# A list scheduler for the w_in stage: other durations, merges of both directions together, and another order of the last gMLP blocks

## The chip, the cores and the metric

The kernel runs on one NeuronCore of a Trainium2 chip, as one program. The metric is the device time of one execution in microseconds (us), here the median of three runs. Everything is computed in fp32; large products are made of three products of split operands (type fp32r, high and low part), small ones are plain fp32.

## The reference, cut to what matters

The reference is one layer of a backbone for 640 tokens (512 latent, 128 context) with a width of 2048. The change lies in the part that makes `p = h @ w_in` and turns its columns into the inputs of a later scan and into the gated spatial unit.

```python
h = _rmsnorm(x, lp['norm1_g']) * (1.0 + sc1) + sh1
p = h @ lp['w_in']
o_a, s_fin = _rwkv7_bidir(shift_fn(p[..., :C_SHIFT], lp['mu_shift']), s0, lp)
o_b = _chunk_gmlp(jax.nn.gelu(p[..., C_SHIFT:]), lp)
x = x + g1 * (jnp.concatenate([o_a, o_b], axis=-1) @ lp['w_out'])
...
def _chunk_gmlp(p, lp):
    u, v = jnp.split(p, 2, axis=-1)
    v = v.astype(F32).reshape(B, T // CHUNK, CHUNK, N_GROUPS_B, HEAD_B)
    mean = jnp.mean(v, axis=-1, keepdims=True)
    vc = v - mean
    v = vc * lax.rsqrt(jnp.mean(vc * vc, axis=-1, keepdims=True) + LN_EPS) * lp['gmlp_ln_g'] + lp['gmlp_ln_b']
    s = jnp.einsum('gij,bnjgd->bnigd', lp['w_spatial'], v) + lp['b_spatial'].T[:, :, None]
    return (u * s.reshape(B, T, D_B)).astype(dtype)
```

`_rwkv7_bidir` is a delta-rule scan over the tokens, forward and backward, for 16 heads of 64. The kernel does it in chunks of 64 tokens: within a chunk it needs the inverse of a triangular 64x64 matrix for each head, direction and chunk. `_chunk_gmlp` has 8 groups of 128 columns for the value `v` and 8 for the gate `u`.

## The kernel before, in words

The program has four stages: the first modulation and norm with the first three column blocks of w_in (up to some 150 us); the rest of w_in with everything that hangs on its columns (the stage of this change); the scan over chunks together with the product with w_out; and the feed-forward part.

**The w_in stage.** The columns of w_in come in blocks of 128. Three are done earlier; 40 remain: for each of 8 pairs of heads the blocks r, v and k, and for each of 8 gMLP groups a value block (`take_gv`) and a gate block (`take_gu`). A block is 96 "wide" products of 128x128 by 320 columns (`wides`, from line 1180): 16 parts of the contraction, two halves of the tokens, three products each (high by high, high by low, low by high). `fetch` loads raw weights on SP, three buffers ahead; `parted` splits them into `hi` on ACT and `lo` on DVE. A finished block is copied to an SBUF buffer `praw` (a ring of four) and given to the queue of its kind.

**What hangs on a block.** `take_r`, `take_v`, `take_k` shift the tokens and build the decays, `R` and `X`; `take_v` also writes the turned values through a tile `vt` to DRAM. `tail` makes the chunk products (`pG`, 64x64 tiles), `turned_x` and `first_z` (`pXT`, `pW`) write more of the scan's records `d_S`. `solve` inverts 16x16 triangles on DVE; `merge` (line 1030) puts them together to 32x32 and then to 64x64 in five steps for each direction: three `pblk` products, `pM` and `pT`, each a group of 20 or 40 products of 32x32 tiles on PE, followed by copies on ACT or additions on DVE. There are 8 merges, so 80 such steps. The result `TF` is stored by a DMA on the POOL queue. `take_gv` does the gelu, turns the value block and `w_spatial`, normalises over 128 columns (mean, variance, root, gain and bias) into `vt`; `take_gu` does the gelu of the gate block, multiplies `vt` by the turned `w_spatial` (`psp`), adds the bias, multiplies and stores `d_o`. `mod_all` makes the remaining modulation vectors in 64 groups of four products (`pm`, 128x32 tiles), paced by the count of wides.

**Who sets the order.** `Lister` (from line 231) writes the order of every engine's instructions at build time. Each queue is a task that yields operations; an `Op` has a cost in microseconds (from line 89). `Lister` keeps a clock for every engine, works out when a task's next operation would be ready, and emits the one that could start first. On PE (`pick`) the wides are the filling. A small product of the full 128x128 shape is taken as soon as it has been ready for SLACK; one of another tile shape interrupts the wides if two small ones are ready for SLACK, or if one has waited for PATIENCE (2 us). Off the full shape, others that are ready for SLACK go along. A change of shape costs 0.195 us on the list's clock. Priorities: r, v, k, tails 2, merges 3, solve 4, gMLP (`qB`, one queue, one block after another) and `mod_all` 5. The list fixes only the order; on the chip each instruction waits for its inputs.

**At the end of the stage.** The main list ends with the last wide. What is left in the queues is emitted by `plan.run(last=True)` outside the hand-made order, where the framework orders it among the first instructions of the next stage. That stage starts with transposes of x (`pxT`), the first scan steps (`swap`, `w_ps`, `u_ps`, `s_ps`, `y_ps`) and products with w_out. PSUM has four slots for small products in this stage (`slots`); `slots.pair` waits for two.

Of the kernel before, what the change touches and what calls it, by code (L numbers as in the profile page):

```python
# [19 lines left out]
P = 128  # L20
# [5 lines left out]
CH = 64  # L26
# [26 lines left out]
SLACK = 1.0  # L53
# [35 lines left out]
class Op:  # L89
# [14 lines left out]
    def __init__(self, eng, name, fn, args, kw):  # L104
# [126 lines left out]
class Lister:  # L231
# [10 lines left out]
    def add(self, gen, prio):  # L242
        self.tasks.append(Task(gen, prio))
# [39 lines left out]
    def pick(self, eng, tasks):  # L283
        now = self.clock[eng]
        c = [(self.ready(t.item), t.rank(), i, t) for i, t in enumerate(tasks)]
        if eng == "PE":
# [8 lines left out]
            if small and (not wide or len(small) >= TOGETHER or now - min(small)[0] >= PATIENCE):  # L295
# [23 lines left out]
def flow_step(ctx: ExitStack, tc, x_prompt, x_sample, state_rwkv, c, c_ctx, w_mod, b_mod,  # L319
# [420 lines left out]
    pairs = [Pair() for _ in range(NPAIR)]  # L740

# [6 lines left out]
    def take_v(pr, p, read):  # L748
# [198 lines left out]
    def take_gv(vv, g, read):  # L947
        lng, lnb, wsp = (gs.tile([P, P], F32, tag=n, name=n) for n in ("lng", "lnb", "wsp"))
        yield oQ.dma_start(lng, gmlp_ln_g[0, g].partition_broadcast(P))
        yield oQ.dma_start(lnb, gmlp_ln_b[0, g].partition_broadcast(P))  # L950
# [17 lines left out]
        va = gs.tile([P, NT], F32, name="gva")  # L968
# [61 lines left out]
    def merge(p, d2):  # L1030
# [6 lines left out]
        for h in range(2):  # L1037
            base = 64 * (1 - h)
            for d in range(2):
                yield oS.copy(A1_[base:base + 16, d, :, 16:32], GB[d][base:base + 16, :, 16:32])  # L1040
                yield oS.copy(A1_[base + 32:base + 48, d, :, 16:32], GB[d][base + 32:base + 48, :, 48:64])
        for d in range(2):
            GBd = GB[d]
            TF = bp.tile([P, NCH, CH], F32, tag="TF", name="TF")
            for h in range(2):
                yield oG.memset(TF[hi32(h), :, 0:32], 0.0)
            Tn, TT, A1 = TB[:, d, :, 0, :], TB[:, d, :, 1, :], A1_[:, d]

            def blk(lhs, rhs, rows=range(4)):
                ps = slots.tile([P, NCH, 32], F32, "pblk")  # L1050
                four = []
                for cc in range(NCH):
                    for a_ in rows:
                        s = slice(32 * a_, 32 * a_ + 32)
                        four.append(oT.matmul(ps[s, cc, :], lhs[s, cc, :], rhs[s, cc, :], start=True, stop=True,
                                             tile_position=(32 * a_, 32 * a_)))
                return ps, four

            M1 = bp.tile([P, NCH, 32], F32, tag="M1", name="M1")
            yield slots.free  # L1060
            ps, four = blk(A1, Tn)
            yield four
            yield oS.copy(M1, ps)
            slots.done(ps)

            yield slots.free
            ps, four = blk(TT, M1, (0, 2))
            yield four
            for h in range(2):
                yield oV.tensor_add(Tn[lo32(h)], ps[lo32(h)], Tn[lo32(h)])  # L1070
            slots.done(ps)
            yield slots.free
            ps, four = blk(M1, TT)
            yield four
            for h in range(2):
                yield oV.tensor_add(TF[lo32(h), :, 0:32], ps[lo32(h)], TT[lo32(h)])
                yield oV.tensor_add(TF[hi32(h), :, 32:64], ps[hi32(h)], TT[hi32(h)])
            slots.done(ps)
            M2 = bp.tile([P, NCH, 32], F32, tag="M1", name="M2")
            yield slots.free  # L1080
            ps = slots.tile([P, NCH, 32], F32, "pM2")
            yield [oT.matmul(ps[hi32(h), cc, :], GBd[lo32(h), cc, 32:64], Tn[lo32(h), cc, :],
                            start=True, stop=True, tile_position=(64 * (1 - h), 64 * (1 - h) + 32))
                   for cc in range(NCH) for h in range(2)]
            for h in range(2):
                yield oS.copy(M2[hi32(h), :, :], ps[hi32(h), :, :])
            slots.done(ps)
            yield slots.free
            ps = slots.tile([P, NCH, 32], F32, "pT2")
            yield [oT.matmul(ps[lo32(h), cc, :], M2[hi32(h), cc, :], TF[hi32(h), cc, 32:64],  # L1090
                            start=True, stop=True, tile_position=(64 * (1 - h) + 32, 64 * (1 - h)))
                   for cc in range(NCH) for h in range(2)]
            for h in range(2):
                yield oS.copy(TF[lo32(h), :, 32:64], ps[lo32(h), :, :])
            slots.done(ps)
# [1111 lines left out]
```

## Time and profile before

| | |
|---|---|
| median of 3 runs | 3248.74 us (3248.45 to 3251.41) |
| the profiled execution | 3247.45 us, its span 3244.2 us |
| granted clock of TensorE, mean | 0.983 |
| busy in the span: PE, DVE, ACT, POOL | 3107.5, 2333.3, 1446.0, 1260.9 us |
| instructions | 73519 |
| the w_in stage (list) | 155 to 1016 us of the span |
| first product of the next stage | 1035.20 us |

A row of the order of time reads: start, length in us, engine, line, operation, tile written <- tiles read, shapes, count, and in brackets the idle time of the engine ahead of it and what ended it. PE counts an fp32 product as two instructions. All operations of the list carry line 106, where they are run, so tiles tell them apart. Matmuls overlap: their distance is read from their starts.

### The profile page before, as it was taken

Reading aid. Unit: us, or ns where it says so; the run is one execution under the profiler, and the core shown is the slowest. Engines: PE = TensorE matmul, PEld = TensorE weight load, DVE = VectorE, ACT = ScalarE, POOL = GpSimd, SP = SyncE. Lnnn points to the kernel's source line nnn. Section 1 sums busy time; section 2 is a strip of 40 time slices with the busy share of each in tenths; the row PEclk is TensorE's granted clock in tenths of the full one; section 3 lists DMA queues with packets and bytes.
Section 4 is the critical chain, followed back from the end, with each engine's and each line's share of the span. In section 5 each row is a group of like instructions: output and inputs, shape, how many; then the busy total and the mean of one; then the engine's idle time right before and its main releaser. Section 6 shows DMA issues by size and latency. Waiting matters only on the chain. (4 is left out here: it accounts for less than half of the span.)

```text
span 3244.2 us, 73519 instructions
## 1 busy us (share of the span) xinstructions
PE 3107.5 (96%) x28828; PEld 2877.5 (89%) x28828; DVE 2333.3 (72%) x4073; ACT 1446.0 (45%) x3161; POOL 1260.9 (39%) x1082
## 2 busy tenths in 40 slices
PE   5899999999998999898999999999999999999996
PEld 3698888889886877788999999999999999999986
DVE  4456767767666666547977877877877777777787
ACT  3244554555543333345644444444444444444365
POOL 0001222222220122301365666566666645555543
PEclk8899999999997999999999999999999999999998
DMA  8768788887896777455434434434433354554353
GB/s 319 254 183 237 212 224 212 237 233 192 230 233 191 215 222 226 136 152 175 123 108 130 125 105 128 127 107 123 123 116 118 110 180 151 160 160 141 110 170 119
DMA packets 741922, 553.00 MB, mean 170 GB/s; under 512 B 141688, under 2 KB 674184, under 8 KB 732744
## 3 DMA queue, kind: packets, MB, share of 16 engines
q1 hardware_dynamic: 729256, 534.62, 55.5%
q0 software_dynamic: 9984, 13.13, 1.7%
q8 instruction: 226, 3.70, 0.5%
q14 instruction: 120, 0.98, 0.1%
q10 hardware_dynamic: 2336, 0.57, 0.1%
HBM read 438.77 MB, written 111.69 MB: 170 GB/s over the span
## 5 line engine op out<-in xcount | busy, mean ns | idle before, releaser
L1819 PE MATMUL P<-xo,lo 128*128 128x320 f32 x2352 | 727.1, 309 | 3.5 <-DVE lo L1636 3.5
L1818 PE MATMUL P<-xo,hi 128*128 128x320 f32 x2352 | 727.6, 309 | 0.0
L1817 PE MATMUL P<-xo,hi 128*128 128x320 f32 x2352 | 727.6, 309 | 0.0
L1636 DVE TENSOR_TENSOR lo<-raw,hi 128x512 fp32r<-128x512 f32 x532 | 514.4, 974 | 162.0 <-ACT hi L1635 159.6
L1635 ACT CAST hi<-raw 128x512 fp32r<-128x512 f32 x532 | 330.2, 622 | 505.6 <-PE P L1818 435.6
L1819 PEld LDWEIGHTS P<-xo,lo 128*128 128x128 f32 x2352 | 441.6, 188 | 4.3 <-DVE lo L1636 4.2
L1818 PEld LDWEIGHTS P<-xo,hi 128*128 128x128 f32 x2352 | 442.3, 188 | 0.0
L1817 PEld LDWEIGHTS P<-xo,hi 128*128 128x128 f32 x2352 | 442.3, 188 | 0.0
L1730 POOL TENSOR_TENSOR raw<-raw 128x512 f32<-128x512 f32 x252 | 413.6, 1645 | 13.6 <-DVE lo L1636 0.6
L106 PE MATMUL big<-h_hi,hi 128*128 128x320 f32 x1280 | 417.8, 326 | 0.9 <-ACT praw L1209 0.9
L1819 PE MATMUL P<-xd,lo 128*128 128x320 f32 x1232 | 384.4, 312 | 16.8 <-DVE lo L1636 16.2
L106 PE MATMUL big<-h_lo,hi 128*128 128x320 f32 x1280 | 394.1, 308 | 0.0
L106 PE MATMUL big<-h_hi,lo 128*128 128x320 f32 x1280 | 394.1, 308 | 0.0
L1817 PE MATMUL P<-xd,hi 128*128 128x320 f32 x1232 | 381.9, 310 | 5.1 <-ACT hi L1635 3.0
L1818 PE MATMUL P<-xd,hi 128*128 128x320 f32 x1232 | 380.7, 309 | 0.0
L1730 POOL TENSOR_TENSOR t<-raw 128x512 f32<-128x512 f32 x84 | 129.5, 1542 | 454.8 <-DMA raw<-in_w_ffn_up_dram 407.5
L1635 ACT CAST hi<-rawd 128x512 fp32r<-128x512 f32 (+1 forms) x288 | 168.7, 588 | 237.9 <-PE P L1818 198.5
L106 PEld LDWEIGHTS big<-h_hi,hi 128*128 128x128 f32 x1280 | 240.7, 188 | 32.6 <-issue 25.9
L1819 PEld LDWEIGHTS P<-xd,lo 128*128 128x128 f32 x1232 | 231.2, 188 | 25.6 <-DVE lo L1636 25.6
L106 PEld LDWEIGHTS big<-h_lo,hi 128*128 128x128 f32 x1280 | 240.7, 188 | 1.2
L106 PEld LDWEIGHTS big<-h_hi,lo 128*128 128x128 f32 x1280 | 240.1, 188 | 0.0
L1817 PEld LDWEIGHTS P<-xd,hi 128*128 128x128 f32 x1232 | 231.4, 188 | 8.6 <-ACT P L2116 4.8
(370 smaller groups left out, 6268.3 us busy)
## 6 DMA issues: line engine op xcount, KB each, us to landing
wt<-in_w_mod_dram SPq DMA_DIRECT2D x96, 1024.0 KB
raw<-in_w_ffn_gate_dram SPq DMA_DIRECT2D x182, 256.0 KB
raw<-in_w_ffn_up_dram SPq DMA_DIRECT2D x182, 256.0 KB
rec<-d_S SPq DMA_DIRECT2D x80, 576.0 KB
raw<-in_w_in_dram SPq DMA_DIRECT2D x172, 256.0 KB
rawd<-in_w_ffn_down_dram SPq DMA_DIRECT2D x128, 256.0 KB
raw<-in_w_out_dram SPq DMA_DIRECT2D x96, 256.0 KB
xd<-d_os SPq DMA_DIRECT2D x66, 320.0 KB
```

The source lines that it names most:

```text
L106: self.eng, self.run = eng, lambda: fn(*args, **kw)
L1635: S.copy(hi[:, 0:nk], raw[:, 0:nk])
L1636: V.tensor_sub(lo[:, 0:nk], raw[:, 0:nk], hi[:, 0:nk].bitcast(F32))
L1730: G.tensor_tensor(out=o[:, 0:nk], in0=p[:, 0:nk], in1=q[:, 0:nk], op=ALU.subtract)
L1817: TE.matmul(ps, hi[:, k, :], xk[:, 0, :], start=f, stop=False)
L1818: TE.matmul(ps, hi[:, k, :], xk[:, 1, :], start=False, stop=False)
L1819: TE.matmul(ps, lo[:, k, :], xk[:, 0, :], start=False, stop=l)
```

## The change

- The costs of PE operations in `Op`: a plain fp32 product takes `n / 600` us over its share instead of `n / 1200`, with other least values; transposes and fp32r products keep theirs.
- `SLACK` goes from 1.0 to 1.5. Each task has its own patience; all values given are 2.0, the old constant.
- `merge` does each of its five steps for both directions in one group, with two PSUM slots; `M1` and `M2` hold both directions, and there are two `TF` tiles, the second in the buffer of `take_v`'s `vt`. A list `held` keeps the two users of that buffer apart.
- The last four gMLP blocks come in the order value 6, value 7, gate 6, gate 7 instead of value 6, gate 6, value 7, gate 7. Group 7 gets buffers of its own for `vt` and `wspT` (those of tiles that are done by then; it waits until all eight `take_k` are through). The bias `lnb` is loaded behind the copy of the turned `w_spatial`, into that matrix's buffer.

```diff
@@ -50,7 +50,10 @@
-SLACK = 1.0
+SLACK = 1.5
+PACE = 2.0
+PATM = 2.0
+PATT = 2.0
@@ -126,8 +129,14 @@
             self.tiling = (q(lhs.shape[0]), q(lhs.shape[1])) if name == "matmul" else (P, P)
             n = math.prod(rhs.shape[1:])
             share = P * P // (self.tiling[0] * self.tiling[1])
-            least = {1: 0.108, 4: 0.05, 16: 0.016}[share] if self.tiling != (P, 32) else 0.08
-            self.cost = max(least, (n / 2400 + 0.0133 if rhs.dtype == F32R else n / 1200) / share)
+            if name == "transpose":
+                self.cost = max(0.109, n / 1200)
+            elif rhs.dtype == F32R:
+                self.cost = max(0.108, n / 2400 + 0.0133)
+            else:
+                where = kw.get("tile_position")
+                least = {1: 0.22, 4: 0.05 if self.tiling != (P, 32) else 0.08, 16: 0.015}[share]
+                self.cost = max(least if not where or where[0] == where[1] else 0.028, n / 600 / share)
@@ -212,8 +221,8 @@
-    def __init__(self, gen, prio):
-        self.gen, self.prio, self.item, self.over = gen, prio, None, False
+    def __init__(self, gen, prio, patience=0.0):
+        self.gen, self.prio, self.patience, self.item, self.over = gen, prio, patience, None, False
@@ -239,8 +248,8 @@
-    def add(self, gen, prio):
-        self.tasks.append(Task(gen, prio))
+    def add(self, gen, prio, patience=PATIENCE):
+        self.tasks.append(Task(gen, prio, patience))
@@ -292,7 +301,7 @@
-            if small and (not wide or len(small) >= TOGETHER or now - min(small)[0] >= PATIENCE):
+            if small and (not wide or len(small) >= TOGETHER or any(now - x[0] >= x[3].patience for x in small)):
@@ -738,6 +747,7 @@
+    held = []
@@ -751,9 +761,12 @@
         o.zv = bk.tile([P, T], F32, tag="zv", name="zv", bufs=1)
         yield from shifted(o.zv, pr, 16 + p)
         read()
+        yield lambda: not held
+        held.append(p)
         vt = bp.tile([P, NT, P], F32, tag="vt", name="vt", bufs=1)
         yield from turned(o.zv, vt, "pvt")
         yield oQ.dma_start(d_vt[p, 0].rearrange("(q t) v -> t q v", t=P), vt)
+        held.pop()
         yield oQ.dma_start(c3(d_vt[p, 1]), c3(d_vt[p, 0])[:, ::-1])
@@ -945,18 +958,21 @@
     vts = [None] * 8
     def take_gv(vv, g, read):
-        lng, lnb, wsp = (gs.tile([P, P], F32, tag=n, name=n) for n in ("lng", "lnb", "wsp"))
+        lng, wsp = (gs.tile([P, P], F32, tag=n, name=n) for n in ("lng", "wsp"))
         yield oQ.dma_start(lng, gmlp_ln_g[0, g].partition_broadcast(P))
-        yield oQ.dma_start(lnb, gmlp_ln_b[0, g].partition_broadcast(P))
         yield oQ.dma_start(wsp, w_spatial[0, g])
         yield from gelu2(vv)
         yield slots.free
         pw = slots.tile([P, 4, P], F32, "pw")
         yield oT.transpose(pw[:, 0, :], wsp, ident)
-        wspT = gs.tile([P, P], F32, name="wspT")
+        wspT = (bk if g == 7 else gs).tile([P, P], F32, tag="wlr" if g == 7 else "wspT", name="wspT", bufs=1)
         yield oS.copy(wspT, pw[:, 0, :])
         slots.done(pw)
-        vt = bp.tile([P, NT, P], F32, tag="vt2", name="vt2", bufs=1)
+        lnb = gs.tile([P, P], F32, tag="wsp", name="lnb")
+        yield oQ.dma_start(lnb, gmlp_ln_b[0, g].partition_broadcast(P))
+        if g == 7:
+            yield lambda: done["zv"] == NPAIR
+        vt = bp.tile([P, NT, P], F32, tag="t2" if g == 7 else "vt2", name="vt2", bufs=1)
         yield from turned(vv, vt, "pvt2")
         bc = lambda ap: ap.unsqueeze(2).to_broadcast([P, NT, P])
         mn = gs.tile([P, NT], F32, name="gmn")
...
-        va = gs.tile([P, NT], F32, name="gva")
+        va = gs.tile([P, NT], F32, tag="gmn", name="gva")
@@ -1039,62 +1055,65 @@
...
+        Tn, TT = ([TB[:, d, :, w, :] for d in range(2)] for w in range(2))
+        M1 = bp.tile([P, 2, NCH, 32], F32, tag="M1", name="M1")
+        TF = [None] * 2
+        two = lambda: [slots.tile([P, NCH, 32], F32, "pblk") for d in range(2)]
+
+        def blk(ps, lhs, rhs, rows=range(4)):
+            return [oT.matmul(ps[d][s, cc, :], lhs[d][s, cc, :], rhs[d][s, cc, :], start=True, stop=True,
+                             tile_position=(s.start, s.start))
+                    for d in range(2) for cc in range(NCH) for s in (slice(32 * a_, 32 * a_ + 32) for a_ in rows)]
+
+        yield slots.pair
+        ps = two()
+        yield blk(ps, [A1_[:, d] for d in range(2)], Tn)
         for d in range(2):
+            yield oS.copy(M1[:, d], ps[d])
+            slots.done(ps[d])
+        yield slots.pair
+        ps = two()
+        yield blk(ps, TT, [M1[:, d] for d in range(2)], (0, 2))
+        for d in range(2):
             for h in range(2):
+                yield oV.tensor_add(Tn[d][lo32(h)], ps[d][lo32(h)], Tn[d][lo32(h)])
+            slots.done(ps[d])
+        yield lambda: not held
+        held.append(p)
+        TF = [bp.tile([P, NCH, CH], F32, tag=n, name="TF", bufs=1) for n in ("TF", "vt")]
+        for d in range(2):
             for h in range(2):
+                yield oG.memset(TF[d][hi32(h), :, 0:32], 0.0)
+        yield slots.pair
+        ps = two()
+        yield blk(ps, [M1[:, d] for d in range(2)], TT)
+        for d in range(2):
             for h in range(2):
+                yield oV.tensor_add(TF[d][lo32(h), :, 0:32], ps[d][lo32(h)], TT[d][lo32(h)])
+                yield oV.tensor_add(TF[d][hi32(h), :, 32:64], ps[d][hi32(h)], TT[d][hi32(h)])
+            slots.done(ps[d])
+        M2 = bp.tile([P, 2, NCH, 32], F32, tag="M1", name="M2")
+        yield slots.pair
+        ps = two()
+        yield [oT.matmul(ps[d][hi32(h), cc, :], GB[d][lo32(h), cc, 32:64], Tn[d][lo32(h), cc, :],
+                        start=True, stop=True, tile_position=(64 * (1 - h), 64 * (1 - h) + 32))
+               for d in range(2) for cc in range(NCH) for h in range(2)]
+        for d in range(2):
             for h in range(2):
+                yield oS.copy(M2[hi32(h), d], ps[d][hi32(h), :, :])
+            slots.done(ps[d])
+        yield slots.pair
+        ps = two()
+        yield [oT.matmul(ps[d][lo32(h), cc, :], M2[hi32(h), d, cc, :], TF[d][hi32(h), cc, 32:64],
+                        start=True, stop=True, tile_position=(64 * (1 - h) + 32, 64 * (1 - h)))
+               for d in range(2) for cc in range(NCH) for h in range(2)]
+        for d in range(2):
             for h in range(2):
+                yield oS.copy(TF[d][lo32(h), :, 32:64], ps[d][lo32(h), :, :])
+            slots.done(ps[d])
+            yield oG.dma_start(d_S[p, :, d, :, F_T:F_T + CH], TF[d])
             merged.append(p)
+        held.pop()
         yield oG.memset(TB[:, :, :, 0, 0:16], 0.0)
@@ -1136,9 +1155,12 @@
         block(2 * DA + P * p, take_v, p, qR)
         block(DA + P * p, take_k, p, qA)
         while g < GORD[p]:
-            block(CSH + DA + P * g, take_gv, g, qB)
-            block(CSH + P * g, take_gu, g, qB)
-            g += 1
+            both = (g, g + 1) if g == 6 else (g,)
+            for u in both:
+                block(CSH + DA + P * u, take_gv, u, qB)
+            for u in both:
+                block(CSH + P * u, take_gu, u, qB)
+            g += len(both)
@@ -1224,13 +1246,13 @@
-        plan.add(queue(qT), 2)
+        plan.add(queue(qT), 2, PATT)
-        plan.add(queue(qM), 3)
+        plan.add(queue(qM), 3, PATM)
-        plan.add(mod_all(), 5)
+        plan.add(mod_all(), 5, PACE)
```

More of the change, by code (lines that the diff above doesn't have):

```diff
@@ L1041, in merge @@
                 yield oS.copy(A1_[base + 32:base + 48, d, :, 16:32], GB[d][base + 32:base + 48, :, 48:64])
-        for d in range(2):
-            GBd = GB[d]
-            TF = bp.tile([P, NCH, CH], F32, tag="TF", name="TF")
-            for h in range(2):
[L1046 to L1068, printed above, removed]
-            for h in range(2):
[L1070 to L1074, printed above, removed]
-            for h in range(2):
[L1076 to L1084, printed above, removed]
-            for h in range(2):
[L1086 to L1092, printed above, removed]
@@ L1093, in merge @@
+        yield slots.pair
[4 more added lines that the diff above has]
+        for d in range(2):
             for h in range(2):
-                yield oS.copy(TF[lo32(h), :, 32:64], ps[lo32(h), :, :])
-            slots.done(ps)
-            yield oG.dma_start(d_S[p, :, d, :, F_T:F_T + CH], TF)
+                yield oS.copy(TF[d][lo32(h), :, 32:64], ps[d][lo32(h), :, :])
+            slots.done(ps[d])
+            yield oG.dma_start(d_S[p, :, d, :, F_T:F_T + CH], TF[d])
```

## The prediction

> **What bounds the kernel now.** I read the table of stretches first, because the change touches one stage alone: the list of the w_in stage (from 155 us, where the hand-ordered blocks take over, to 1016 us) and its hand-over to the next stage. Columns: stretch, its length, busy time of PE, PEld, DVE, ACT and POOL with instruction counts, PE clock, DMA share, GB/s.
>
> ```profile
> 155.00:1016.00 861.00, 854.91 (x11325) 753.34 (x11323) 583.77 (x1222) 424.46 (x922) 188.78 (x298) 1.00 0.80 216
> 1016.00:1020.00 4.00, 1.18 (x6) 0.92 (x6) 3.29 (x6) 3.10 (x7) 1.00 (x1) 0.88 0.86 212
> 1020.00:1035.00 15.00, 3.02 (x13) 2.36 (x11) 10.56 (x17) 4.30 (x7) 1.18 (x1) 0.50 0.85 282
> 1035.00:1051.00 16.00, 15.68 (x129) 11.35 (x129) 6.50 (x20) 6.01 (x21) 0.00 (x0) 0.50 0.79 239
> 1055.00:1075.00 20.00, 20.00 (x144) 19.65 (x143) 9.89 (x24) 4.45 (x9) 0.00 (x0) 1.00 0.73 221
> ```
>
> Two regimes. Up to 1016 us PE is busy 854.9 of 861 us; DVE has 277 us free and ACT more. From 1016 to 1035 us PE does almost nothing, and the 16 us behind that are PE-bound at half clock. A stage saves time only by less PE work before 1016, or by a shorter hole behind it. Whether PE really never waits is read from its waits in the stage (who waited for whom, total, times, longest):
>
> ```profile
> PE pblk L106 <- issue: 2.0, 2, 1.4
> PE pm L106 <- DMA wt<-in_w_mod_dram: 1.5, 2, 0.8
> PE pmm L106 <- ACT Z L106: 1.1, 1, 1.1
> PE pG L106 <- issue: 1.0, 1, 1.0
> PE pmm L106 <- DVE fs L106: 0.3, 1, 0.3
> ```
>
> That is 5.9 us in all. So the list has almost no waiting to win on PE; its price is in the products and in what lies between them. The wide products, by the groups of lines in this stretch:
>
> ```profile
> L106 PE MATMUL big<-h_hi,hi 128*128 128x320 f32 x1268 | 414.0, 326 | 0.0
> L106 PE MATMUL big<-h_hi,lo 128*128 128x320 f32 x1269 | 390.7, 308 | 0.0
> L106 PE MATMUL big<-h_lo,hi 128*128 128x320 f32 x1268 | 390.5, 308 | 0.0
> ```
>
> Their durations overlap, so I take the distance of starts from the order of time. One step of a merge (pblk, 32x32 tiles), alone between wides, and one beside a product of the modulation (pm):
>
> ```profile
> 970.71 0.31 PE L106 MATMUL big<-h_lo,hi 128*128 128x320 f32 x1
> 970.86 0.30 PE L106 MATMUL big<-h_hi,lo 128*128 128x320 f32 x1
> 971.10 0.89 PE L106 MATMUL pblk<-TB,A__1111 32*32 32x32 f32 x80
> 971.91 0.41 PE L106 MATMUL big<-h_hi,hi 128*128 128x320 f32 x1
> 972.16 0.31 PE L106 MATMUL big<-h_lo,hi 128*128 128x320 f32 x1
> ...
> 997.01 0.31 PE L106 MATMUL big<-h_hi,lo 128*128 128x320 f32 x1
> 997.25 0.89 PE L106 MATMUL pblk<-TB,A__1111 32*32 32x32 f32 x80
> 998.07 1.04 PE L106 MATMUL pm<-wt,cT 128*2 128x512 f32 x8
> 999.04 0.42 PE L106 MATMUL big<-h_hi,hi 128*128 128x320 f32 x1
> ```
>
> Wide to wide is 0.147 us (970.71 to 970.86 and its neighbours). 3805 wides by 0.147 make 559 us; the other 302 us of the 861 are small products with their changes of tile shape.
>
> **Merges of both directions in common groups.** The lone step costs 972.16 - 970.86 = 1.30, less two wides, 1.01 us. Its 80 instructions themselves need 0.89 less the length of one (operations of a tile, with least, median and longest ns; between them the first and the last merge step that I counted alone in the order of time):
>
> ```profile
> L106 PE MATMUL pblk<-TB,A__1111 x1280: 184/191/212, 353.5 to 997.9; 32*32 32x32 f32 x183
> ...
> 410.13 0.82 PE L106 MATMUL pM<-TB,GB 32*32 32x32 f32 x40
> ...
> 1014.70 0.82 PE L106 MATMUL pT<-TF,M 32*32 32x32 f32 x40
> ...
> L106 PE MATMUL pm<-wt,cT x512: 591/592/593, 156.8 to 998.5; 128*2 128x512 f32 x171
> ```
>
> 0.89 - 0.19 = 0.70 us. So leaving the wide shape and coming back costs 0.31; in company (997.25 to 998.07, 0.82) the step pays 0.12. The products stay the same in number; the change makes 40 steps of the 80 (8 pairs, 2 directions, 5 steps). Of the 80 I counted 21 alone in a visit, from 410.13 to 1014.70, and 59 in company. Removing 40 in that proportion: 10.5 x 0.31 + 29.5 x 0.12 = 6.8 us. Copies and additions on ACT and DVE stay in number. Each step now asks for two of the four PSUM slots at once, as the tails do; if it waits for them, wides go on, so I cost it at nothing. The second TF tile takes over vt's buffer, and a list of holders makes take_v and the second half of a merge wait for each other: five steps of some 4 us (997.25 to 1014.70 for the last merge's five), three of them holding. What queues behind that is the r and v queue, and its praw buffer has been given back ahead of the wait; I cost it at nothing, cover being the ring of four blocks, and at up to one block's stall if the cover is gone (inside the slow rival).
>
> **SLACK 1.0 to 1.5, patience per task.** All three patiences are 2.0 like the old constant, so those change nothing. With SLACK 1.5 a second small step must be half a microsecond older before it triggers a common visit: fewer pairs. Ten more visits alone at 0.31 - 0.12 cost 1.9 us, none costs 0, thirty cost 5.7. Against that, older inputs remove part of the 5.9 us of waits (none to 4). I take +2 and -1: together 1 us dearer, bounds -4 and +6.
>
> **Durations of full fp32 products.** They cost nothing on the chip: they only move steps in the list. The old formula gives a pm group 4 x 512/1200/4 = 0.43 us, the new one 0.85; the chip takes 998.07 to 999.04, 0.97 us with the way out, so the new one is nearer. 64 such groups (512 instructions, two to a product, four products to a group) are 27 us of PE time that the old list did not know of, besides smaller ones. In the new list the other engines get through more between two wides. Where that matters is the lowest queue, gMLP's, at the end.
>
> **The hole behind the last wide.** Last wide and the gMLP chain in the order of time, ACT, DVE, SP and PE:
>
> ```profile
> 982.19 0.74 ACT L106 ACTIVATE gq<-praw 128x640 f32<-128x640 f32 x1 [3.21 <-DVE praw L106]
> 995.00 0.41 ACT L106 COPY praw<-big 128x320 f32<-128x320 f32 x1
> 999.59 0.83 DVE L106 TENSOR_TENSOR vt<-vt,lnb 128x640 f32<-128x640 f32 x1
> 1000.60 0.74 ACT L106 ACTIVATE gq<-praw 128x640 f32<-128x640 f32 x1
> 1015.17 0.74 ACT L106 ACTIVATE gq<-praw 128x640 f32<-128x640 f32 x1 [1.93 <-DVE praw L106]
> 1015.41 0.42 SPq L106 DMA_DIRECT2D d_o<-praw  x1
> 1016.12 0.30 PE L106 MATMUL pw<-ident,wsp 128*128 128x128 f32 x1
> 1016.68 0.41 ACT L106 COPY praw<-big 128x320 f32<-128x320 f32 x1
> 1019.25 1.09 PE L106 MATMUL pvt<-ident,praw 128*128 128x128 f32 x4 [2.83 <-DVE praw L106]
> 1030.90 0.82 DVE L106 TENSOR_TENSOR vt<-vt,lnb 128x640 f32<-128x640 f32 x1
> 1031.87 2.47 PE L106 MATMUL psp<-wspT,vt 128*128 128x128 f32 x10 [11.32 <-DVE vt L106]
> 1034.25 0.89 DVE L106 TENSOR_TENSOR sp<-psp,bsp 128x512 f32<-128x512 f32 x2
> 1035.18 0.83 DVE L106 SCALAR_TENSOR_TENSOR praw<-praw,sp 128x640 f32<-128x640 f32 x1
> 1035.20 1.12 PE L1537 MATMUL pxT<-ident,x1T 128*128 128x128 f32 x4 [0.86 <-DVE sp L106]
> ```
>
> Value block 6 runs from 982.19 to 1000.4 (18.2 us), gate block 6 from 1000.60 to its store at 1015.41 (14.8), value block 7 only from 1015.17, though its data lay ready at 995.41. So this queue is 20 us in arrears, and swapping two blocks in it does not by itself shorten it. What the swap does: behind the last wide then stand gate blocks, which have no normalisation. One needs the gelu (1015.17 to 1019.25, 4.1 us), the sum (0.89) and the product (0.83), 5.8 us, against 1015.17 to 1031.72 for the value block. The next stage's first PE instruction waits for the last sum (0.86 us behind DVE at 1035.20).
>
> My sum: the last wide ends 6 us earlier (6.8 less 1), about 1010.3. If the arrears stay, value block 7 ends at 1000.4 + 18.2 = 1018.6, two gates less the last product add 10.8, and the restart is at 1029.4, 5.8 us early. If the new durations make up 8 of the 27 us for this queue, value block 7 is done with the last wide, and the restart is at 1010.3 + 10.8 = 1021.1, 14.1 early. If they make up 14 or more, one gate is left: its copy ends 1.0 behind the last wide (1017.09 now), and 1010.3 + 1.0 + 5.0 = 1016.3, 18.9 early. I take the middle one: its 8 us are a third of the 27. The moved lnb load waits on SP for the copy of wspT; behind it stand the w_in loads, three buffers ahead; I cost it at nothing, bounds 0 and 2 us. The store of the last block keeps its place as the last of the list, and the loads behind it on SP move with it. Everything from 1055 us on is PE-bound and just moves. 14 us off the profiled execution's 3247.45 is 3233; its time lies 1.3 under the median of 3248.74, so the median becomes 3234.
>
> **The clock in the hole.** The 16 us from 1035 were at half clock with PE 98% busy; at full clock they would be about 8. The transposes at 1019.25, behind only 2.83 us of idling, were already slow (4 in 1.09 us). So I expect the new hole, shorter but above 2.8 us, to leave PE cold as before: no gain in the sum. [...]
>
> **Rivals.** *Warm or caught up* (chance 0.18): one gate left, and PE stays warm or wakes early. 19 us and up to 8 more: 3222 to 3230. For it: gate block 6 took 14.8 us where 5.8 would do on quieter engines, so there is much to make up. Against: the cold transposes.
> *A shuffled backlog* (0.20): arrears stay and the PE saving vanishes in front of them; 0 to 6 us early, 3243 to 3249. For it: a serial queue has the same sum in any order. This is also the case where the change does not do what it says.
> *The list loses its margin* (0.12), the slower side: the missing PE time was a hidden reserve, which gave each small step's input some time to arrive. With true durations PE, in order, meets steps whose copy from ACT or DVE is not there and waits, with all wides queued behind it. One such wait costs 0.8 us (longest of the two pm waits). It decides from 14/0.8 = 18 waits on: with 40 of the stage's small steps it is 32 us, less 14: 3267. Against: the old list has seven waits, and SLACK adds 0.5 us to each step.
>
> **Numbers.** Forecast 3234 at 0.50, its own range 3228 to 3242. What a measurement of this kernel can tell from no change is 0.2%, 6.5 us. Faster: 0.50 + 0.18 and a little of the backlog, 0.70; same 0.18; slower 0.12. The range 3220 to 3249 takes in the first three cases and leaves the slow one out.
>
> **What would show it.** Merge steps in 40 visits of 160 instructions, and the last wide near 1010; PE waits in the stage still under 10 us; behind the last wide no transposes of a value block, and pxT near 1021; the stretch from there to the first wide of w_out as long as now and at 0.50. Wrong it is if the last wide lies at or behind 1016, if PE's waits have grown past 14 us, or if a value block still stands behind the last wide.

## The result and the profile after

The changed kernel takes 3288.98 us in the median of four runs (3284.09 to 3292.82), the kernel before 3249.7 us on the same chip. The ratio is 1.0115 (95% interval 1.0097 to 1.0133): 39 us slower, where 3234 us was forecast and 3249 was the upper end of the range. The profiled execution took 3292.82 us, its span 3290.8 (before: 3247.45 and 3244.2).

The table of stretches of the changed kernel, with the columns as before: the list up to its last wide, the hole in two parts, the restart up to the first product with w_out, and a stretch further on.

```profile
155.00:1062.00 907.00, 867.13 (x11321) 763.52 (x11320) 586.84 (x1221) 428.90 (x927) 190.36 (x300) 0.98 0.77 205
1062.00:1066.00 4.00, 2.51 (x24) 2.35 (x23) 3.89 (x9) 0.94 (x2) 0.00 (x0) 1.00 0.13 25
1066.00:1078.80 12.80, 0.51 (x6) 0.32 (x4) 8.79 (x15) 3.55 (x5) 0.00 (x0) 0.63 0.69 201
1078.80:1090.50 11.70, 9.55 (x57) 6.43 (x57) 2.47 (x7) 4.38 (x10) 0.00 (x0) 0.50 0.93 297
1095.00:1115.00 20.00, 20.00 (x142) 19.72 (x141) 10.83 (x27) 3.85 (x7) 0.00 (x0) 0.96 0.61 193
```

The list does the same number of products (11321 where there were 11325; here and below a product is one that PE counts, two for each fp32 product of the program) and needs 907 us for them instead of 861; the last wide starts at 1061.84 instead of 1015.84. PE is idle for 40 us of it (907.00 less 867.13) where it was idle for 6, and its clock, which was 1.00, is 0.98. The whole loss lies in the list: the span is 46.6 us longer, the last wide 46.0 us later. PE's waits in the list, by who waited for whom:

```profile
PE pblk L109 <- issue: 29.8, 12, 4.9
PE pm L109 <- DMA wt<-in_w_mod_dram: 5.2, 6, 2.1
PE big L109 <- issue: 2.0, 1, 2.0
PE pG L109 <- issue: 0.9, 1, 0.9
PE pw L109 <- DMA wsp<-in_w_spatial_dram: 0.9, 1, 0.9
```

29.8 us stand ahead of merge products and have no other engine as their releaser: "issue" means that nothing shown in the profile was awaited. The merge was 2.0 us of such time before. One of these stops in the order of time:

```profile
1015.41 0.31 PE L109 MATMUL big<-h_hi,lo 128*128 128x320 f32 x1
1015.65 0.32 PE L109 MATMUL pblk<-TB,A__1111 32*32 32x32 f32 x6
1016.61 1.42 PE L109 MATMUL pblk<-TB,A__1111 32*32 32x32 f32 x142 [0.64 <-DMA TB<-d]
1022.94 0.42 PE L109 MATMUL pblk<-TB,A__1111 32*32 32x32 f32 x12 [4.91 <-issue]
1023.29 0.64 PE L109 MATMUL big<-h_hi,hi 128*128 128x320 f32 x1
1023.72 0.47 PE L109 MATMUL big<-h_lo,hi 128*128 128x320 f32 x1
1023.99 0.47 PE L109 MATMUL big<-h_hi,lo 128*128 128x320 f32 x1
```

PE stops 12 products before the end of a group of 160, whose operands were all there, and goes on 4.91 us later. Behind it the wides start 0.27 us apart (1023.72 to 1023.99) instead of 0.147: PE has fallen to half clock (the trace has a granted clock of 0.50 from 1021.49 to 1028.31). What came in during the stop, from the view of the DMA queues for 1017.84 to 1022.94 us (packets, MB, share of 16 engines' time):

```profile
DMA packets 836, 1.51 MB, mean 297 GB/s; under 512 B 55, under 2 KB 627, under 8 KB 716
...
q1 hardware_dynamic: 835, 1.50, 97.2%
q8 instruction: 1, 0.02, 1.4%
```

One packet of instructions among 835 packets of data, on DMA engines that are full (97.2%). The trace records for it a start at 1020.29 and 1.18 us; PE goes on 1.47 us after its end. This isn't one case: in the changed list all 14 stops under "issue" end 1.2 to 1.5 us behind the end of such a packet, and so do the three in the list before, although the packets come only every 10 us (89 in the 907 us). Between the starts of the packet before (997.91) and of this one the trace has 540 products and weight loads of PE. The page of the changed kernel counts these packets:

```profile
PE 3125.7 (95%) x28828; PEld 2890.8 (88%) x28828; DVE 2343.6 (71%) x4073; ACT 1448.2 (44%) x3161; POOL 1259.4 (38%) x1082
...
q8 instruction: 226, 3.70, 0.5%
```

28828 products and as many weight loads are 57656 instructions; divided by 226 packets they are 255 to a packet, of 16384 bytes in the trace. 540 is more than two packets. A joint merge group of 160 products is 320 instructions: more than a packet, used up in 1.5 us (1.39 us from the first start to the last in groups without a wait). Of the 40 joint groups 16 have 160 products and 24 have 80; nine of the twelve stops ahead of merge products stand in groups of 160, three (6.6 us) in groups of 80. So the theory to test: **PE runs out of instructions**. Its rivals are that such a group waits for its data or PSUM slots, that its length alone stops PE, and that the list itself became worse (the durations, SLACK, the order).

### The profile page after: what moved, and what is told of

The parts are those of the page before. It is cut to its first block, busy times and chain, and to the rows that moved or that the text cites. A ratio compares the mean times of both kernels' runs of the same rounds, so it can differ in the third digit from the quotient of the medians.

```text
span 3290.8 us, 73523 instructions
## 1 busy us (share of the span) xinstructions
PE 3125.7 (95%) x28828; PEld 2890.8 (88%) x28828; DVE 2343.6 (71%) x4073; ACT 1448.2 (44%) x3161; POOL 1259.4 (38%) x1082
## 5 line engine op out<-in xcount | busy, mean ns | idle before, releaser
L1658 DVE TENSOR_TENSOR lo<-rawd,hi 128x512 fp32r<-128x512 f32 (+1 forms) x288 | 228.4, 799 | 26.8 <-ACT hi L1657 22.6
```

Of the source, the lines that this page charges most:

```text
L1658: V.tensor_sub(lo[:, 0:nk], raw[:, 0:nk], hi[:, 0:nk].bitcast(F32))
```

## The experiments

The table gives the ratio to the kernel before, and from each profiled execution: waits of PE from 155 us to the last wide ("issue", and all others), the start of the last wide, and how far behind it the next stage's first transposes (pxT) and the scan's first step (swap) start.

| kernel | ratio (95%) | issue us | others us | last wide | pxT | swap | span |
|---|---|---|---|---|---|---|---|
| before | | 3.0 | 2.9 | 1015.8 | +19.4 | +20.4 | 3244.2 |
| changed | 1.0115 (1.0097 to 1.0133) | 32.7 | 6.9 | 1061.8 | +16.9 | +23.2 | 3290.8 |
| 1 merges alone | 1.0077 (1.0060 to 1.0094) | 18.9 | 4.3 | 1032.5 | +29.7 | +31.8 | 3267.7 |
| 2 changed, groups parted | 1.0057 (1.0042 to 1.0072) | 4.0 | 17.1 | 1041.8 | +8.2 | +20.9 | 3267.9 |
| 3 changed, old merge | 1.0035 (1.0021 to 1.0049) | 1.2 | 15.4 | 1036.9 | +7.0 | +19.7 | 3267.2 |
| 4 changed, old costs | 1.0094 (1.0076 to 1.0113) | 22.6 | 6.2 | 1040.6 | +30.4 | +36.7 | 3283.4 |
| 5 order alone | 1.0032 (1.0019 to 1.0045) | 1.6 | 6.7 | 1016.3 | +39.3 | +26.8 | 3259.7 |
| 6 durations and SLACK | 1.0023 (1.0014 to 1.0033) | 2.5 | 7.8 | 1027.1 | +11.7 | +23.2 | 3260.5 |
| 7 durations alone | 1.0022 (1.0010 to 1.0034) | 5.4 | 11.5 | 1033.7 | +7.3 | +20.0 | 3257.5 |
| 8 groups issued twice | one run, 3360.93 us | 51.8 | 8.3 | 1132.4 | +9.1 | +20.7 | 3358.7 |
| 9 old merge, SLACK 3 | 1.0054 (1.0034 to 1.0074) | 0.0 | 10.2 | 1020.4 | +28.4 | +21.7 | 3256.7 |
| 10 changed, thin loads | 1.0043 (1.0028 to 1.0058) | 15.7 | 1.7 | 1029.7 | +16.0 | +22.3 | 3256.9 |
| 11 order, modulation first | 0.9995 (0.9985 to 1.0004) | 0.4 | 8.2 | 1020.1 | +9.4 | +20.9 | 3247.5 |
| 12 modulation first alone | 0.9994 (0.9983 to 1.0006) | 2.4 | 4.6 | 1013.6 | +27.4 | +20.0 | 3241.9 |

The variants' times scatter by 5 to 20 us from execution to execution; a profile is one draw (that of run 3 is its slowest time, that of run 9 its fastest). So sizes are read from the ratios, and mechanisms from the profiles.

Not every expectation was met. The times of runs 1, 4, 6, 7, 10 and 12 lie where one of the named theories had them. Runs 2, 3, 5 and 9 were slower than their theory by 9, 2, 10 and 15 us, although in runs 2 and 3 the waits within groups fell as expected. Run 8 stopped for 52 us where 10 to 30 were expected, and took 46 us more than the upper end of what was expected. Run 11 has the hole of its theory and the time of its rival; the hole of run 12 (27.4 us) is longer than expected.

**1. The merges alone**, put into the kernel before with the buffers that they need; costs, SLACK and order as before.

```diff
...
+        yield slots.pair
+        ps = two()
+        yield blk(ps, [A1_[:, d] for d in range(2)], Tn)
...
-        lng, lnb, wsp = (gs.tile([P, P], F32, tag=n, name=n) for n in ("lng", "lnb", "wsp"))
+        lng, wsp = (gs.tile([P, P], F32, tag=n, name=n) for n in ("lng", "wsp"))
```

> The kernel before with the joint merges alone (durations, SLACK and the order of the gMLP blocks as before; only the buffers that the second TF tile needs are shared as in the change). Theory F (instruction fetch): PE's own instructions come in packets of 16384 bytes, 256 of them to a packet by 3.70 MB over its 57,656 products and weight loads, and a joint group runs through up to 320 within 1.5 us, so PE stops inside the group until a packet has come. Then this kernel waits as the changed one: 20 to 40 us in all inside groups of pblk, 3270 to 3295 us. Theory M (lost margin, as the slow rival of the prediction): with the old durations the waits are gone, and the joint groups save some 7 us: 3235 to 3248 us.

3272.78 us, by the ratio 25 us slower. The stops are there without any other part of the change, fewer ahead of merge products than expected (11.9 us) and some ahead of other small products:

```profile
PE pblk L106 <- issue: 11.9, 6, 3.6
PE pG L106 <- issue: 4.6, 2, 2.7
PE pvt L106 <- issue: 2.2, 1, 2.2
```

**2. The changed kernel with each joint group parted into one group for each direction**; everything else of the change stays.

```diff
...
-        yield slots.pair
-        ps = two()
-        yield blk(ps, [A1_[:, d] for d in range(2)], Tn)
         for d in range(2):
-            yield oS.copy(M1[:, d], ps[d])
-            slots.done(ps[d])
+            yield slots.free
+            ps, four = one(A1_[:, d], Tn[d])
+            yield four
+            yield oS.copy(M1[:, d], ps)
+            slots.done(ps)
...
```

> The changed kernel with each joint group parted again: the same buffers, the same step for both directions one behind the other, but one group per direction with its copy in between, so that wides come between the groups. Theory F: waits inside the groups fall from 32 us to under 8, time 3238 to 3258 us. Theory M: durations and SLACK are those of the change, so the waits stay: 3275 to 3292 us.

3267.42 us. "Issue" falls from 32.7 to 4.0 us: with the groups parted, nearly all the stops are gone. What remains is another loss, waits for data:

```profile
PE pm L109 <- DMA wt<-in_w_mod_dram: 7.1, 5, 2.2
PE pblk L109 <- DMA TB<-d: 5.5, 3, 3.2
PE pblk L109 <- issue: 3.3, 2, 1.8
```

**3. The changed kernel with the old merge and take_v**; durations, SLACK 1.5 and the order stay.

```diff
...
-        yield lambda: not held
-        held.append(p)
...
+            yield slots.free
+            ps, four = blk(A1, Tn)
+            yield four
+            yield oS.copy(M1, ps)
...
```

> The changed kernel with the whole merge as before (one direction behind the other, one TF tile, no holders): durations, SLACK and the order of the gMLP blocks stay. Theory F: 3235 to 3255 us, waits inside groups under 6 us. Theory M: 3270 us or more.

3257.05 us; "issue" 1.2 us, other waits 15.4. By the ratios the loss of 37 us (1.0115) has become one of 11 (1.0035).

**4. The changed kernel with the old durations and SLACK 1.0.**

```diff
-SLACK = 1.5
+SLACK = 1.0
...
+            least = {1: 0.108, 4: 0.05, 16: 0.016}[share] if self.tiling != (P, 32) else 0.08
+            self.cost = max(least, (n / 2400 + 0.0133 if rhs.dtype == F32R else n / 1200) / share)
```

> The changed kernel with the old durations and SLACK 1.0; joint merges and the order of the gMLP blocks stay. Theory F: waits inside pblk groups stay at 20 to 40 us, 3270 to 3295 us. Theory M: the waits are gone, 3230 to 3250 us.

3278.98 us. Other waits are back at 6.2 us, "issue" stays at 22.6: the stops don't come from the costs.

**8. The dose raised in the kernel before**: each pblk group is issued twice into the same places, so that groups have up to 320 instructions. Those products are done twice, and the result is the same.

```diff
-                return ps, four
+                return ps, four + [oT.matmul(ps[slice(32 * a_, 32 * a_ + 32), cc, :], lhs[slice(32 * a_, 32 * a_ + 32), cc, :],
+                                             rhs[slice(32 * a_, 32 * a_ + 32), cc, :], start=True, stop=True,
+                                             tile_position=(32 * a_, 32 * a_)) for cc in range(NCH) for a_ in rows]
```

> The kernel before, durations, SLACK, order and merges as they were, but each pblk group issues its products twice (the second time over the first, with the same result): up to 320 PE instructions in one group without two PSUM slots, holders or a second TF tile. The products cost 16 x 2 x 0.70 + 16 x 0.63, some 33 us of PE time by themselves. Theory F: on top of that PE stops inside the groups for its own instructions, 10 to 30 us in all, each stop ending 1.2 to 1.6 us behind the end of a packet of the instruction queue; 3290 to 3315 us. Rival P (the stops came from the pair of PSUM slots, the holders or the shared buffers): inside the groups under 4 us, 3275 to 3285 us.

```profile
PE pblk L106 <- issue: 37.9, 17, 3.8
PE big L106 <- issue: 6.9, 4, 3.9
```

The stops grow from 3.0 to 51.8 us in a kernel with no other part of the change. Its page also says whose the packets of q8 are:

```profile
PE 3176.6 (95%) x32028; PEld 2936.2 (87%) x32028; DVE 2341.2 (70%) x4073; ACT 1448.7 (43%) x3161; POOL 1258.8 (37%) x1082
...
q8 instruction: 251, 4.11, 0.5%
```

3200 products and 3200 weight loads more, and 25 packets more: 256 instructions to a packet.

**10. The changed kernel with less data beside its instructions**: the same written order of PE, instruction for instruction. It leaves out most of the modulation's weights, so its output is another number and only its time is of use.

```diff
...
+                m = 16 if kb else P
+                load = oQ.dma_start(quad[:m].rearrange("p j n -> p (j n)"), w_mod[0, kb * P:kb * P + m, g * D:(g + 1) * D])
+                load.bytes *= P // m
+                yield load
```

> The changed kernel in which 60 of the 64 loads of the modulation weights bring 16 partitions of 128 instead of all (the products then use stale weights, so the modulation and all that hangs on it is another number). 52 MB less are moved in the stage; the order of every product on PE is the same as in the changed kernel. Theory (PE runs out of instructions, whose packets wait among the data on the 16 DMA engines): the packets land sooner, the stops of PE that end behind an instruction packet fall from 36 us (15 stops) to 8 to 20 us, the half-clock time in the list from 37.5 us to under 20, and the last wide comes 20 to 40 us earlier than in the changed kernel; median 3250 to 3272. Rival one (a joint group stops PE by itself, by its length, whatever the DMA engines do): the stops stay at 30 to 40 us, the last wide stays within 8 us of 1062, median 3278 to 3290 (5 us less for the waits of pm for its weights, which go in either case). Rival two (a joint group stops for its data, TB or M1): nothing in the list's stops changes, as those inputs do not come by these loads.

3262.92 us, by the ratios 23 us faster than the changed kernel; "issue" falls from 32.7 to 15.7 us, and the share of the DMA engines in the list from 0.77 to 0.64. The stop shown above is there again, at the same product, but shorter:

```profile
987.69 1.42 PE L109 MATMUL pblk<-TB,A__1111 32*32 32x32 f32 x142 [0.79 <-DMA TB<-d]
991.69 0.42 PE L109 MATMUL pblk<-TB,A__1111 32*32 32x32 f32 x12 [2.58 <-issue]
```

Seven more stops stand at the same product of the same group in both traces (behind 150, 143, 154, 119, 139, 134 and 141 of 160), as they must if the ends of packets make them. The instruction packets land sooner, as expected, but not because they take less time themselves (median 1.09 us, with full loads 1.03): they start sooner. Counted from the start of the last product ahead of the stop, the packet for the stop behind product 119 starts 2.41 us later with full loads and 0.61 us earlier with thin ones; for the one shown, 2.45 and 0.03 us later. Some 5 of the 32 us by which the last wide comes sooner are another gain: `pm` no longer waits for its weights (other waits 1.7 us instead of 6.9). Rival one, length alone, falls with this: the groups have kept their length. Data and slots fell with run 8, which changed neither.

**6 and 7. The durations, with SLACK 1.5 and alone**, in the kernel before. Run 6 has both lines of this diff and the cost formula, run 7 the formula only.

```diff
-SLACK = 1.0
+SLACK = 1.5
...
+                self.cost = max(least if not where or where[0] == where[1] else 0.028, n / 600 / share)
```

> The kernel before with the new durations and SLACK 1.5 alone; merges and block order as before. Theory M2 (the true durations take the margin out of the list): PE's waits for data (pm on its weights from DRAM, first products on copies) go from 7 to 15 us or more and the last wide comes 8 to 20 us later, while the hole behind it is shorter by 5 us or more, since the other engines are further on: 3250 to 3262 us. If the durations do no harm: last wide within 4 us of before, 3238 to 3249 us. Theory F expects waits inside pblk groups under 4 us either way.

> The kernel before with the new durations of full fp32 products alone: SLACK stays 1.0, merges, order and buffers as before. Before with durations and SLACK together cost 0.23% and lengthened the list by 19 us, 15 us of it waits of PE. If the durations are what takes the margin from the list (my rival of the lost margin as written): waits of 10 us or more remain, the list ends at 1026 to 1036, median 3253 to 3262. If it is SLACK 1.5 that reorders the list for the worse: waits stay under 9 us, the list ends before 1024, median 3244 to 3252.

3256.29 and 3257.36 us: the durations cost 7 to 8 us, SLACK nothing that can be told. In the profile of run 6 the last wide comes 11.3 us later than before and PE's waits sum to 10.3 us, less than the 19 and 15 that the expectation of run 7 names. PE's waits in run 7:

```profile
PE pm L106 <- DMA wt<-in_w_mod_dram: 7.8, 4, 3.7
PE pG L106 <- issue: 2.7, 2, 1.4
PE pblk L106 <- issue: 2.7, 2, 1.6
PE pXT L106 <- DVE GA L106: 2.6, 1, 2.6
```

This is the rival of the lost margin: steps whose input used to be there are now waited for, 11.5 us in seven waits instead of 2.9 in four. At the same time the gMLP queue does catch up, and the restart comes 7.3 us behind the last wide instead of 19.4.

**9. Run 3 with SLACK 3.0**, to give the margin back.

```diff
-SLACK = 1.5
+SLACK = 3.0
```

> The kernel with new durations and new gMLP order and the old merges (as e3), but SLACK 3.0, so that each small product must have been ready for 3 us on the list's clock. Theory M2: PE's waits for data fall from 16 to under 8 us, the last wide comes 8 us or more earlier than in e3, while the hole behind it stays short: 3238 to 3252 us. If the waits are not a matter of margin (a DMA that is late by its own queue), they stay above 12 us and the time within 5 us of e3's.

The last wide is back at 1020.4 in the profile, but pxT comes 28.4 us behind it, and the median is 3267.46. In this profile what the list wins the hand-over loses again; no single wait accounts for the median, and why it is the slower one stays open.

**5. The order alone**, with its buffers, in the kernel before.

```diff
...
+            both = (g, g + 1) if g == 6 else (g,)
+            for u in both:
+                block(CSH + DA + P * u, take_gv, u, qB)
+            for u in both:
+                block(CSH + P * u, take_gu, u, qB)
+            g += len(both)
```

> The kernel before with the last gMLP blocks in the new order alone (and the buffers that this needs). Theory B (backlog): with the old durations the gMLP queue is in arrears at the end whatever its order, so the next stage still starts 16 us or more behind the last wide: 3243 to 3252 us. Rival O (the order shortens the hole by itself): the next stage starts within 10 us of the last wide, 3234 to 3243 us. PE's waits in the list as before, under 10 us.

3261.95 us, by the ratio 10 us slower, with the last wide where it was. DVE's last gate product and PE's rows behind the last wide:

```profile
1026.23 0.83 DVE L106 SCALAR_TENSOR_TENSOR praw<-praw,sp 128x640 f32<-128x640 f32 x1
```

```profile
1039.64 1.89 PE L106 MATMUL pm<-wt,cT 128*2 128x512 f32 x8 [7.42 <-DMA wt<-in_w_mod_dram]
1043.08 0.69 PE L1357 MATMUL swap<-I,s 64*64 64x64 f32 x8 [1.56 <-DMA s<-in_state_rwkv_dram]
...
1046.73 1.89 PE L106 MATMUL pm<-wt,cT 128*2 128x512 f32 x8 [1.89 <-DMA wt<-in_w_mod_dram]
1054.04 1.08 PE L106 MATMUL ptm<-ident,ms 128*128 128x128 f32 x4 [5.42 <-DMA x1T<-in_x_sample_dram]
1055.57 1.09 PE L1543 MATMUL pxT<-ident,x1T 128*128 128x128 f32 x4 [0.44 <-DVE modc L106]
```

The two gates are through 10 us behind the last wide, as forecast for them (10.8). But the modulation has slipped: its last groups load and multiply behind the last wide, and pxT waits for `modc`.

**11 and 12. The modulation at priority 3 instead of 5**, in run 5 (11) and in the kernel before (12).

```diff
-        plan.add(mod_all(), 5)
+        plan.add(mod_all(), 3)
```

> The kernel before with the new order of the last gMLP blocks and its buffers, and with the modulation products at priority 3 instead of 5 in the list. In the order alone (priority 5) the two gates were done at 1026.2, 9.8 us behind the last wide, as my prediction had it (10.8), but the restart waited until 1055.57 for the modulation: three pm groups stood behind the last wide. In the written order of this kernel all pm groups stand ahead of the last wide and only the two gates behind it. Theory (the order pays what I forecast once the modulation isn't last): last wide within 6 us of 1016, restart 9 to 13 us behind it, waiting for sp; median 3236 to 3246. Rival (a serial queue has the same sum in any order): restart 16 us or more behind the last wide, or the last wide itself at 1022 or later, because another step has lost its place; median 3247 to 3258.

> The kernel before with the modulation products at priority 3 instead of 5, nothing else: what the priority does by itself. Its written order still has a value block behind the last wide. Theory: list and hole as before within 6 us (last wide 1010 to 1022, restart 17 to 21 us behind it), median 3244 to 3256. If it is the priority and not the order that shortens the hole, the restart comes within 13 us of the last wide and the median is under 3243.

Run 11 does in the hole what the change was to do: pxT comes 9.4 us behind the last wide and waits for `sp`. Still it is no faster (0.9995). Nor is run 12 slower (0.9994), whose hole is 27.4 us. The stretches from the last wide over the restart to about the 400th product with w_out, of the kernel before and of run 11:

```profile
1016.10:1035.20 19.10, 4.10 (x18) 3.27 (x17) 13.92 (x23) 7.30 (x14) 2.18 (x2) 0.58 0.84 265
1035.20:1051.00 15.80, 15.68 (x129) 11.35 (x129) 6.33 (x19) 6.01 (x21) 0.00 (x0) 0.50 0.80 242
1051.00:1193.30 142.30, 141.59 (x1922) 117.98 (x1921) 89.17 (x277) 53.71 (x225) 23.61 (x33) 0.99 0.70 213
```

```profile
1020.30:1029.50 9.20, 3.33 (x62) 3.06 (x61) 7.38 (x14) 5.04 (x9) 1.00 (x1) 0.90 0.67 207
1029.50:1044.90 15.40, 11.18 (x62) 7.09 (x62) 3.66 (x8) 6.21 (x14) 0.00 (x0) 0.50 1.04 323
1044.90:1195.90 151.00, 150.53 (x1988) 124.33 (x1988) 93.96 (x292) 54.59 (x233) 23.59 (x33) 0.97 0.70 215
```

The hole is 9.9 us shorter. But in the restart PE does 62 products where it did 129, and the others follow in the long stretch, which is 8.7 us longer; the sums are 177.2 and 175.6 us. Early or late, pxT seems to be only filling: the scan's first step comes 20.4 us behind the last wide in the kernel before and 20.9 in run 11. In the table it stays at 19.7 to 23.2 in nine of the twelve kernels with an edit and in the changed one, while pxT moves from 7.0 to 28.4. In run 12 the trace names what it waits for, its loads:

```profile
1033.65 0.69 PE L1351 MATMUL swap<-I,s 64*64 64x64 f32 x8 [4.95 <-DMA s<-in_state_rwkv_dram]
```

In the others the step stands in line behind pxT, and that its loads would hold it there too is argued, not shown. SP issues the first of these loads 6.8 us behind the last wide in the kernel before and 11.6 us behind it in run 11; the step starts 9.3 us behind that issue in run 11, 8.7 in run 12, where it waits for them, but 5.0 in the changed kernel, where it doesn't. So in run 11 they may have been the limit or not.

## Why the prediction was wrong

**The joint merges (the step that failed).** I counted 80 steps becoming 40, 6.8 us saved, and put down the longer groups at nothing, because the products "stay the same in number". I priced PE's shape changes, slots and data, and not the supply of its instructions, although the page of before had the line on q8 and the number of instructions. The term that I put at nothing is 29.7 us of "issue" (32.7 less 3.0), and a second one hangs on it: the clock, granted at 0.50 in 37.5 us of the changed list and in none of the list before. 68 wides in the changed list start 0.26 to 0.275 us apart instead of 0.147, 12 in the one before: 56 by 0.12 are 6.7 us. With 4.0 us more of other waits that is 40 of the 46; for the other 6 no run shows the cause. The saving itself may be real: in run 1 the list, counted from its first wide, is 15.8 us longer, of which "issue" is 15.9, other waits 1.4 and slow wides 3.8 (32 by 0.12), which leaves minus 5.3. That is one profile, and no run shows the saving by itself.

**The durations.** "They cost nothing on the chip" failed: 1.0022 in run 7. The rival of the lost margin had the mechanism (its chance was 0.12), but a smaller size: 11.5 us in seven waits of PE, not 32 in forty. I had let it decide from 18 waits on, because it had 14 us of gain to eat up first; that gain did not exist. That the durations would let the gMLP queue catch up was right.

**SLACK.** 1 us dearer was forecast; runs 6 and 7 differ by nothing that can be told.

**The hole.** Its content came as forecast: two gates and at most the end of a value block behind the last wide, 9.4 us in run 11 where I had 10.8. In the changed kernel it is 16.9, with the same order and gMLP buffers as in run 11, and not by one cause. Counted from the last wide in both: value block 7 ends 1.4 us behind it (1063.25) instead of 1.0 us ahead, and gate 6 is through its gelu 3.3 us later. Its sum (`sp`) then starts 2.4 us after the gelu, right behind an operation of the next stage (`gl`) that stands ahead of it on DVE and had waited 1.68 us. The rest, 1.9 us, is lost in gate 7; 0.80 of it is a wait for its bias:

```profile
1063.28 0.36 SPq L109 DMA_DIRECT2D bsp<-in_b_spatial_dram  x1
1069.51 0.83 DVE L1330 TENSOR_TENSOR gl<-gl,gh 128x640 fp32r<-128x640 f32 x1 [1.68 <-ACT gh L1329]
1070.25 0.88 DVE L109 TENSOR_TENSOR sp<-psp,bsp 128x512 f32<-128x512 f32 x2
1072.40 0.43 SPq L109 DMA_DIRECT2D bsp<-in_b_spatial_dram  x1
1077.85 0.89 DVE L109 TENSOR_TENSOR sp<-psp,bsp 128x512 f32<-128x512 f32 x2 [0.80 <-DMA bsp<-in_b_spatial_dram]
```

The bias comes late because lnb now lives in the buffer that it takes too: gate 6 loads it only when value block 7 is through, gate 7 when gate 6 is. I had looked at what queues behind the moved load, not at who shares its buffer. Whether gate 6 waited for its bias as well can't be told from the trace.

**What the hole is worth.** "Everything from 1055 us on is PE-bound and just moves" failed as well: the sum took pxT as the start of what follows. Shortening the hole by 10 us gained 1.6 us over the three stretches of run 11 and nothing in its median, so of the 14 us of forecast gain the 8 that came from the hole (14.1 less the 6 of the last wide) did not show.

**The clock.** No gain in the hole was right: the restart of the changed kernel ran at 0.50 as before. That stops within the list would cost clock was not in the sum.

## What to carry to other kernels

Count instructions, not only products. Here a group of 320 instructions of small PE products ran in 1.5 us where a packet brought some 255, and with the DMA engines at 97.2% PE stood 4.91 us with all its operands at hand. With the groups parted, so that wides stand between them, "issue" fell from 32.7 to 4.0 us. The sign of it was a wait put down to "issue" in the middle of a group of equal products. And before a hole is shortened, look at which instruction of the next stage sets its end: here the first one came 10 us sooner and nothing was gained.

## What the runs showed of the hardware

**Instructions.** The packets of q8 have 16384 bytes each in the trace. They are 226 for the 57656 products and weight loads of the changed kernel, 255 to a packet, and 25 more for the 6400 more of run 8, 256 to a packet. With groups of 320 instructions in 1.5 us PE stands under "issue" for 32.7 us of the changed list, each stop ending 1.2 to 1.5 us behind the end of such a packet, and for 15.7 us with a smaller load on the DMA engines (their share in the list 0.64 instead of 0.77, run 10).

**The clock.** In the changed list, stops in merge products of 1.26 to 1.68 us left no record of half clock; those of 2.00 to 3.00 us left one of 3.4 or 6.8 us, those of 4.31 to 4.91 us one of 6.8, each beginning between 2.9 us ahead of and 1.0 us behind the end of the stop. The length alone doesn't decide it: two idle times of 2.02 and 2.08 us, ahead of a wide and of a `pm` group, left none. So in the list PE was back at full clock after 3.4 or 6.8 us; in the hand-over the record of half clock is one of 27.3 us in the changed kernel and of 34.1 us in the kernel before.
